# One decoder layer on one core: the last scores of the fourth attention group later, block two's probability transposes in two bursts, block two's MLP norm statistics ahead of the low parts

## The chip, the cores and the metric

The kernel runs on one core of a Trainium2 chip. The metric is the device time of one execution in microseconds (us), median over the runs. Three runs of the kernel before gave 1505.65, 1504.33 and 1505.69 us. The profiled execution took 1504.41 us, and its records span 1502.6 us from the first instruction to the last, so 1.8 us lie around the span.

Five engines work side by side, each through its own queue in order: PE multiplies matrices (its weight loads stand apart as PEld), DVE and ACT work on vectors, POOL is almost unused here, and SP starts transfers. What one needs from another it waits for at a semaphore.

## What is computed

One decoder layer in float32 on 256 tokens of width 2048. Around the change:

```python
h = rmsnorm(x, norm_mix_pre)
xr, yr, q, k, v, g_rnn, g_attn = split(h @ w_in)
y_att = sliding_window_sink_attention(rope(q), rope(k), v, sinks)   # 32 heads of 64, 4 key groups, window 128
mix = sigmoid(g_rnn) * (y_rnn @ w_rnn_proj) + sigmoid(g_attn) * (y_att @ w_attn_proj)
x = x + rmsnorm(mix @ w_out, norm_mix_post)
h = rmsnorm(x, norm_mlp_pre)
x = x + rmsnorm(square(relu(h @ w_mlp_up)) @ w_mlp_down, norm_mlp_post)
```

## The kernel before

**Tiling.** The 256 tokens are two blocks of 128 (`tb` 0 and 1). Float32 products are made of three products in a rounded format: each operand is split into a high part and a low part, and high by high, high by low and low by high are added. Weights stream in halves of 128x1024: SP loads `wraw` (4 buffers), ACT casts the high part `whi` (line 107, or 116 where it is issued by hand), DVE subtracts to get the low part `wlo` (line 108 or 124); `whi` and `wlo` have 6 buffers each. PE multiplies them with the activations: lines 307, 309 and 311 in the passes that keep tokens on the output's partitions, lines 267 and 269 in those that keep channels there (`a_pair`), line 952 for the last steps of `w_out`, line 1024 for the first steps of `w_mlp_up`.

**Attention between the projections.** For each of the four key groups `attention(g, banks)` is a generator. While PE runs the projections that follow, `pump()` is called after each half of weights (in `a_pair` four times a pair) and advances the oldest generator to its next `yield`. So each group's small steps lie between the large matmuls: `scores` (PE, line 579) into PSUM banks, `masked` (DVE, lines 591 and 593) which scales and masks them into SBUF and takes maxima, `exponents` (ACT, line 610), `shares` (DVE, lines 617 to 620) which divides by the sums, `turn_probs` (PE transposes, line 637, into banks `pt`, then ACT copies, line 639), and the product with the values (line 677, into `po`). Groups one to three run under the next group's passes; the fourth runs under `recur(0)`, the first channel passes of the recurrent branch (`conv` from line 738 and `gelu` from line 755, whose PSUM results are read by ACT at line 296 and DVE at line 297).

**Banks.** `pt` has the pool `psm` with two banks. `turn_probs(1)` fills four (two parities by two key blocks, four transposes each), so its third and fourth must wait for the ACT copies of the first two. In the first three groups the second block's scores have four banks; in the fourth, two of those are in use by the channel passes, and the second half of the scores must wait for `masked` to empty the pool `psb`.

**Before the MLP.** `w_out`'s result passes a norm, and `h2` must be transposed for `w_mlp_up`. For block one, then block two: `square` (ACT, line 920) sums squares, `gained` (DVE, line 923) applies gains, `norm` (lines 957 to 962: a reduce on DVE, a root on ACT, a reciprocal and four `h2` quarters on DVE), `turned` (PE transposes, line 968), `high` (ACT, line 973) and `low` (DVE, line 978). Block two's four transposed quarters share two banks, so the third waits until `high` and `low` of the first have read theirs. Meanwhile PE does block one's share of `w_mlp_up` (line 1024) with `whi` halves cast by hand (line 116).

**What sets the order.** A scheduler orders each engine's instructions at build time and the engines then run that fixed order. What is wrapped in `pin` keeps the order in which it was written.

Of the kernel before, what the change touches and what calls it, by code (L numbers as in the profile page):

```python
# [18 lines left out]
F32 = mybir.dt.float32  # L19
# [160 lines left out]
def layer(tc, x, x_t, few, pos_row, gains, w_kv, w_q, w_xy, w_rg, w_g, w_rp, w_ap, w_out,  # L180
# [43 lines left out]
    def unit(name, dt=F32R):  # L224
        return big.tile([P, 4, 2, S], dt, tag="U8", name=name)

    def flat(t):
        return t.rearrange("p a b c -> p (a b c)")

    ws = Stream(nc, wpool, chunks, lambda name: flat(unit(name, F32)), sums)  # L230
# [4 lines left out]
    def bank(pool, name):  # L235
        return pool.tile([P, 512], F32, tag=pool.name, name=name)
# [13 lines left out]
    def pair(name):  # L250

        pool = pairs[0]
        pairs.append(pairs.pop(0))
        return pool.tile([P, 2, 2, S], F32, tag="pair" + pool.name, name=name)
# [69 lines left out]
    def two_banks(name):  # L324
        room = pair(name)
        return [room[:, tb].rearrange("p a b -> p (a b)") for tb in range(TB)]
# [19 lines left out]
    def quarter(q):  # L346
        return slice(q * 512, q * 512 + 512)
# [203 lines left out]
    def attention(g, banks):  # L551
# [13 lines left out]
        rooms, stats, tiles = {}, {}, {}  # L565

        def scores(tb, j, both):

            w = P * (1 + tb)
            per = 512 // w  # L570
            if j == 0:
                rooms[tb] = flat(unit("s", F32)).rearrange("p (n c) -> p n c", c=512)
                stats[tb] = pa.tile([P, 4, 8], F32, tag="stat", bufs=3, name="stat")
                tiles[tb] = []
            for i in range(per):
                h = j * per + i
                for par in range(2):
                    r0 = par * HD
                    pin(mm(both[par][:, i * w : i * w + w], qT[r0 : r0 + HD, h, tb * P : tb * P + P],
                           kT[r0 : r0 + HD, g, 0:w], start=True, stop=True))  # L580
            return tb, j, both
# [40 lines left out]

        pT = {}

        def turn_probs(tb):
            nk = 1 + tb
            per = 4 // nk
            if tb:
                room_p = flat(unit("pT", F32)).rearrange("p (n c) -> p n c", c=512)
            else:  # L630
                room_p = rooms[tb][:, 2:4, :]
            for par in range(2):
                for kb in range(nk):
                    ps = bank(psm, "pt")
                    for h in range(4):
                        s3, at = tiles[tb][h // per * 2 + par]
                        nc.tensor.transpose(ps[:, h * P : h * P + P], s3[:, h % per, kb * P : kb * P + P], ident)
                    t = room_p[:, par * nk + kb, :]
                    nc.scalar.copy(t, ps)
                    pT[tb, par, kb] = t  # L640
# [11 lines left out]
        masked(*two)  # L652
        yield
        if last_group:
            three = scores(1, 1, [bank(psb, "sc") for par in range(2)])
            yield
        masked(*three)
# [6 lines left out]
        exponents(1, (2, 3))  # L664
        yield
        turn_probs(0)
        shares(1)
        yield
        yield
        turn_probs(1)  # L670
        yield
        yield
        for tb in range(TB):
            po = bank(psm, "po")
# [16 lines left out]
    for g in range(NKV):  # L691
        m1.append(pa.tile([P, TB, 512], F32, tag="m1", bufs=4, name=f"m1{g}"))
        for tb, b in enumerate(b_pass512(hT, two_banks("g"), 1)):
            nc.scalar.activation(m1[g][:, tb], b, AF.Tanh, scale=r0h[tb])
        waiting.append(attention(g, b_pass512(hT, [bank(psb, f"q{tb}") for tb in range(TB)], 1)))
# [220 lines left out]
    late = []  # L916
    h2T = units("h2T")

    def square(tb, q, b):
        pin(nc.scalar.activation(u2("j"), b, AF.Square, accum_out=sq[:, 1, tb, q : q + 1]))  # L920

    def gained(tb, q, b):
        pin(nc.vector.tensor_tensor(h2[tb][:, quarter(q)], b, gpg2[:, quarter(q)], ALU.mult))


    banks = [two_banks(f"o0{tb}") for tb in range(TB)]
# [17 lines left out]
    banks = [[bank(psb, f"o1{tb}{i}") for i in range(2)] for tb in range(TB)]  # L944
# [4 lines left out]
    def last_step(tb, i, kt, hi, lo):  # L949
        a, c = mixT[kt // 4][:, kt % 4], quarter(i)  # L950
        for x, w in ((0, hi), (0, lo), (1, hi)):
            pin(mm(banks[tb][i], a[:, x, tb * P : tb * P + P], w[:, c], start=False, stop=kt == KT - 1 and x == 1))

    def norm(tb):

        a, b = [st[:, 4 + 2 * tb + i : 5 + 2 * tb + i] for i in range(2)]
        pin(nc.vector.tensor_reduce(a, sq[:, 1, tb, :], AX.X, ALU.add))
        pin(nc.scalar.activation(b, a, AF.Sqrt, bias=eps, scale=1.0 / D))
        pin(nc.vector.reciprocal(a, b))
        for q in range(4):  # L960
            c = quarter(q)
            pin(nc.vector.scalar_tensor_tensor(h2[tb][:, c], h2[tb][:, c], a, xg[tb][:, c], ALU.mult, ALU.add))
        r1.append(a)

    def turned(tb, q):
        for i in range(4):
            k = 4 * q + i
            pin(nc.tensor.transpose(rooms[tb][q][:, i * P : i * P + P], h2[tb][:, k * P : k * P + P], ident))

    def high(tb, q):  # L970
        t = slice(tb * P, tb * P + P)
        p3 = rooms[tb][q].rearrange("p (a b) -> p a b", a=4)
        order["high"] = pin(nc.scalar.copy(h2T[q][:, :, 0, t], p3)).ins

    def low(tb, q):
        t = slice(tb * P, tb * P + P)
        p3 = rooms[tb][q].rearrange("p (a b) -> p a b", a=4)
        order["low"] = pin(nc.vector.tensor_tensor(h2T[q][:, :, 1, t], p3, h2T[q][:, :, 0, t].bitcast(F32),
                                                   ALU.subtract)).ins

    for i in range(2):
        for h in held:
            last_step(0, i, *h)
        square(0, 2 + i, banks[0][i])
        gained(0, 2 + i, banks[0][i])
    norm(0)
    for i in range(2):

        pin(nc.scalar.copy(og[:, 0, quarter(2 + i)], banks[0][i]))
    rooms = [[r[:, i].rearrange("p a b -> p (a b)") for r in (pair("ptr"), pair("ptr")) for i in range(2)],  # L990
             2 * [bank(psb, f"ptr{i}") for i in range(2)]]
# [5 lines left out]
    begun = [h[0] for h in halves]  # L997
    for h in range(2):
        last_step(1, 1, *held[2 * h])
        for q in (2 * h, 2 * h + 1):  # L1000
            turned(0, q)
        for q in (2 * h, 2 * h + 1):
            high(0, q)
        if h == 0:
            begun.append(ws.split_high())
        last_step(1, 1, *held[2 * h + 1])
        for q in (2 * h, 2 * h + 1):
            low(0, q)
        if h == 0:
            ws.split_low()  # L1010
    square(1, 3, banks[1][1])
    gained(1, 3, banks[1][1])
    begun.append(ws.split_high())
    norm(1)
    for j in range(2):
        begun.append(ws.split_high())


# [29 lines left out]
    for tb in range(TB):  # L1048
        for i in range(2):
            q = 2 + i  # L1050
# [146 lines left out]
    for f in range(2):  # L1197
        uT = {}
        rooms = [unit(f"uT{f}{i}") for i in range((PAIRS - len(SEVEN) + 1) // 2)]
# [48 lines left out]
        def between(p):  # L1248
            if p < 4:
                c = quarter(p)  # L1250
                nc.sync.dma_start(g3[:, c], gains[3][c].partition_broadcast(P))
            if p in (3, 5, 7, 9):
                tb, q = divmod((p - 3) // 2, 2)
                c = quarter(q)
                nc.vector.tensor_tensor(acc[tb][:, c], acc[tb][:, c], g3[:, c], ALU.mult)
# [27 lines left out]
        n = 0  # L1283
        down(f, n, uT, 2, order, finish, early)
        n = 1
# [82 lines left out]
```

## Time and profile before

| what | value |
|---|---|
| runs | 1505.65, 1504.33, 1505.69 us |
| profiled execution | 1504.41 us |
| its span | 1502.6 us |
| granted TensorE clock, mean | 0.997 |
| DVE busy | 1096.6 us (73%) |
| ACT busy | 829.9 us (55%) |
| PE's waits for other engines, summed by the view of waits | 4.9 us in 4 places |

The profile lists, for each instruction, its start from the span's beginning and its busy time. On PE the end of a matmul is modelled and runs into the next one, so the cost of a matmul is the distance from its start to the next start. "x8" merges eight instructions in a row. "Idle before" and an arrow name the engine, tile and line whose work ended the idle time.

### The profile page before, as it was taken

Reading aid. Unit: us, or ns where it says so; the run is one execution under the profiler, and the core shown is the slowest. Engines: PE = TensorE matmul, PEld = TensorE weight load, DVE = VectorE, ACT = ScalarE, POOL = GpSimd, SP = SyncE. Lnnn points to the kernel's source line nnn. Section 1 sums busy time; section 2 is a strip of 40 time slices with the busy share of each in tenths; the row PEclk is TensorE's granted clock in tenths of the full one; section 3 lists DMA queues with packets and bytes.
Section 4 is the critical chain, followed back from the end, with each engine's and each line's share of the span. In section 5 each row is a group of like instructions: output and inputs, shape, how many; then the busy total and the mean of one; then the engine's idle time right before and its main releaser. Section 6 shows DMA issues by size and latency. Waiting matters only on the chain.

```text
span 1502.6 us, 19925 instructions
## 1 busy us (share of the span) xinstructions
PE 1487.6 (99%) x7568; PEld 1259.3 (84%) x7568; DVE 1096.6 (73%) x1356; ACT 829.9 (55%) x1137; POOL 1.7 (0%) x9
## 2 busy tenths in 40 slices
PE   9999999999999999999999999999999999999997
PEld 7887787889889888888888888888888888888886
DVE  6576667858669966555758766798886666789897
ACT  8564664637566666443345654555454555455553
POOL 0000000000000000000000000000000000000000
PEclk9999999999999999999999999999999999999999
DMA  8644554565646566555764755566666565566665
GB/s 339 217 156 159 161 165 131 168 195 176 204 160 215 169 207 203 191 184 194 274 216 144 263 185 194 185 203 211 212 203 242 190 194 185 193 238 207 209 221 176
DMA packets 83471, 298.28 MB, mean 199 GB/s; under 512 B 9264, under 2 KB 9520, under 8 KB 82352
## 3 DMA queue, kind: packets, MB, share of 16 engines
q1 hardware_dynamic: 80064, 289.57, 58.3%
q10 hardware_dynamic: 3312, 7.45, 1.4%
q8 instruction: 59, 0.97, 0.2%
q14 instruction: 36, 0.29, 0.1%
HBM read 290.69 MB, written 6.29 MB: 198 GB/s over the span
## 4 chain that ended last, share of the span: by engine, by line
PE 97%; DVE 2%; ACT 1%; DMA 0%; issue 0%; DVEq 0%; SPq 0%; ACTq 0%
PE ps L269 22%; PE ps L267 12%; PE dQ L1131 9%; PE s L1131 5%; PE dP L1131 4%; PE g L307 4%; PE g L309 4%; PE g L311 4%; PE pp L309 4%; PE pp L307 4%; PE pp L311 4%; PE dCs L1131 3%; PE q L307 2%; PE q L311 2%; PE q L309 2%; PE o L311 2%
## 5 line engine op out<-in xcount | busy, mean ns | idle before, releaser
L108 DVE TENSOR_TENSOR wlo<-wraw,whi 128x1024 fp32r<-128x1024 f32 x516 | 624.2, 1220 | 312.1 <-ACT whi L107 309.5
L107 ACT CAST whi<-wraw 128x1024 fp32r<-128x1024 f32 x516 | 537.9, 1051 | 546.6 <-PE ps L269 132.1
L269 PE MATMUL ps<-h2T,whi 128*128 128x512 f32 x960 | 223.9, 390 | 0.0
L269 PEld LDWEIGHTS ps<-h2T,whi 128*128 128x128 f32 x960 | 178.2, 188 | 35.6
L267 PEld LDWEIGHTS ps<-h2T,wlo 128*128 128x128 f32 x960 | 119.1, 192 | 2.3
L269 PE MATMUL ps<-hT,whi 128*128 128x512 f32 x512 | 120.7, 391 | 0.0
L267 PE MATMUL ps<-h2T,wlo 128*128 128x256 f32 x960 | 119.9, 283 | 0.0
L269 PEld LDWEIGHTS ps<-hT,whi 128*128 128x128 f32 x512 | 94.7, 188 | 19.1 <-issue 0.3
L1131 PE MATMUL dQ<-whi,uT 128*128 128x512 f32 x288 | 106.8, 389 | 0.0
L307 PE MATMUL g<-whi,hT 128*128 128x512 f32 x256 | 101.1, 395 | 0.0
L311 PE MATMUL g<-whi,hT 128*128 128x512 f32 x256 | 99.8, 390 | 0.0
L309 PE MATMUL g<-wlo,hT 128*128 128x512 f32 x256 | 99.7, 390 | 0.0
L267 PEld LDWEIGHTS ps<-hT,wlo 128*128 128x128 f32 x512 | 63.8, 191 | 2.7 <-issue 1.5
L267 PE MATMUL ps<-hT,wlo 128*128 128x256 f32 x512 | 65.2, 284 | 0.0
L1131 PEld LDWEIGHTS dQ<-whi,uT 128*128 128x128 f32 x288 | 54.1, 188 | 11.2
L307 PEld LDWEIGHTS g<-whi,hT 128*128 128x128 f32 x256 | 48.1, 188 | 10.6 <-issue 1.0
L311 PEld LDWEIGHTS g<-whi,hT 128*128 128x128 f32 x256 | 48.1, 188 | 10.2
L309 PEld LDWEIGHTS g<-wlo,hT 128*128 128x128 f32 x256 | 48.1, 188 | 9.6
L1131 PE MATMUL dQ<-wlo,uT 128*128 128x512 f32 x144 | 56.0, 389 | 0.0
L1131 PE MATMUL dP<-whi,uT 128*128 128x512 f32 x144 | 54.1, 389 | 0.0
L1131 PE MATMUL dCs<-whi,uT 128*128 128x512 f32 x144 | 54.1, 389 | 0.0
L143 DVE TENSOR_TENSOR tlo<-t,thi 128x1536 fp32r<-128x1536 f32 x28 | 49.2, 1756 | 5.7 <-ACT thi L142 5.7
(284 smaller groups left out, 2466.5 us busy)
## 6 DMA issues: line engine op xcount, KB each, us to landing
wraw<-in_w_up SPq DMA_DIRECT2D x128, 512.0 KB, 4.1
wraw<-in_w_dn SPq DMA_DIRECT2D x128, 512.0 KB, 4.7
wraw<-in_w_g SPq DMA_DIRECT2D x64, 512.0 KB, 4.7
wraw<-in_w_xy SPq DMA_DIRECT2D x64, 512.0 KB, 3.9
wraw<-in_w_q SPq DMA_DIRECT2D x32, 512.0 KB, 4.1
wraw<-in_w_ap SPq DMA_DIRECT2D x32, 512.0 KB, 4.6
wraw<-in_w_rp SPq DMA_DIRECT2D x32, 512.0 KB, 4.0
wraw<-in_w_out SPq DMA_DIRECT2D x32, 512.0 KB, 4.8
```

Source lines behind the costliest of these rows:

```text
L107: self.pin(self.nc.scalar.copy(hi, src))
L108: self.pin(self.nc.vector.tensor_tensor(lo, src, hi.bitcast(F32), ALU.subtract))
L143: v.tensor_tensor(lo, t, hi.bitcast(F32), ALU.subtract)
L267: mm(ps[:, f, 1, :], w, a[:, 0, :], start=False, stop=j == 1 and k == 7)
L269: mm(ps[:, f].rearrange("p a b -> p (a b)"), w, a.rearrange("p a b -> p (a b)"), start=kt == 0, stop=j == 3 and k == 7)
L307: mm(banks[tb][n], a[:, 0, t], hi[:, n * 512 : n * 512 + 512], start=first, stop=False)
L309: mm(banks[tb][n], a[:, 0, t], lo[:, n * 512 : n * 512 + 512], start=False, stop=False)
L311: mm(banks[tb][n], a[:, 1, t], hi[:, n * 512 : n * 512 + 512], start=False, stop=last)
L1131: mm(b, a[x], w[y], start=not begun and i == 0, stop=tail and i == 2)
```

## The change

Three edits. In the fourth group one more `yield` stands ahead of the last scores. `turn_probs(1)` becomes two calls, one for each parity, with a `yield` between; this holds in all four groups, and the number of yields after it falls by one. Before the MLP, `norm(1)` is given two callbacks: the reduce and the root come ahead of the last `low` of block one, and the last `gained` of block two comes ahead of the last quarter of `h2` alone; the cast that stood ahead of `norm(1)` follows it.

```diff
-        def turn_probs(tb):
+        def turn_probs(tb, pars=(0, 1)):
             nk = 1 + tb
             per = 4 // nk
-            if tb:
-                room_p = flat(unit("pT", F32)).rearrange("p (n c) -> p n c", c=512)
-            else:
-                room_p = rooms[tb][:, 2:4, :]
-            for par in range(2):
+            if tb and 0 in pars:
+                rooms["pT"] = flat(unit("pT", F32)).rearrange("p (n c) -> p n c", c=512)
+            room_p = rooms["pT"] if tb else rooms[tb][:, 2:4, :]
+            for par in pars:
...
         if last_group:
+            yield
             three = scores(1, 1, [bank(psb, "sc") for par in range(2)])
             yield
         masked(*three)
...
-        turn_probs(1)
-        yield
+        turn_probs(1, (0,))
+        yield
+        turn_probs(1, (1,))
         yield
...
-    def norm(tb):
+    def norm(tb, between=None, late=None):
         a, b = [st[:, 4 + 2 * tb + i : 5 + 2 * tb + i] for i in range(2)]
         pin(nc.vector.tensor_reduce(a, sq[:, 1, tb, :], AX.X, ALU.add))
         pin(nc.scalar.activation(b, a, AF.Sqrt, bias=eps, scale=1.0 / D))
+        if between:
+            between()
         pin(nc.vector.reciprocal(a, b))
         for q in range(4):
             c = quarter(q)
+            if q == 3 and late:
+                late()
             pin(nc.vector.scalar_tensor_tensor(h2[tb][:, c], h2[tb][:, c], a, xg[tb][:, c], ALU.mult, ALU.add))
...
-        for q in (2 * h, 2 * h + 1):
-            low(0, q)
+        low(0, 2 * h)
         if h == 0:
+            low(0, 1)
             ws.split_low()
     square(1, 3, banks[1][1])
-    gained(1, 3, banks[1][1])
-    begun.append(ws.split_high())
-    norm(1)
-    for j in range(2):
+    norm(1, lambda: low(0, 3), lambda: gained(1, 3, banks[1][1]))
+    for j in range(3):
         begun.append(ws.split_high())
```

In the first three groups the second burst of eight transposes (line 636 in the new numbering) now stands twelve projection matmuls behind the first, where before two pieces of four stood three and four matmuls behind it.

**The fourth group's last scores on PE** (`sc`, between channel matmuls with low weights at line 267 and high weights at line 269). Before:

```order
L267 MATMUL ps<-hT_150,wlo_2094 128x256 x2
L579 MATMUL sc<-kT,qT_2115 128x256
L267 MATMUL ps<-hT_150,wlo_2094 128x256
L579 MATMUL sc<-kT,qT_2115 128x256 x3
L267 MATMUL ps<-hT_150,wlo_2094 128x256
L267 MATMUL ps<-hT_147,wlo_2133 128x256 x4
L267 MATMUL ps<-hT_148,wlo_2133 128x256 x4
```

Now:

```order
L267 MATMUL ps<-hT_150,wlo_2094 128x256 x4
L267 MATMUL ps<-hT_147,wlo_2133 128x256 x4
L267 MATMUL ps<-hT_148,wlo_2133 128x256 x4
L267 MATMUL ps<-hT_149,wlo_2160 128x256 x4
L267 MATMUL ps<-hT_150,wlo_2160 128x256 x4
L579 MATMUL sc<-kT,qT_2115 128x256 x4
L269 MATMUL ps<-hT_147,whi_2132 128x512 x3
```

The four scores stand together, eighteen line-267 matmuls later than the first stood.

**The fourth group's transposes for block two**, on PE (`pt`) and on ACT (the copies `pT`, lines 639 before and 638 now; `u` and `xct` are the activation of `gelu`, lines 757 and 759 before, 758 and 760 now). PE now; before, the two bursts of eight had a single line-269 matmul between them:

```order
L269 MATMUL ps<-hT_150,whi_2385 128x512 x4
L636 MATMUL pt<-ident,s 128x128 x8
L269 MATMUL ps<-hT_147,whi_2422 128x512
L267 MATMUL ps<-hT_147,wlo_2346 128x256 x4
L267 MATMUL ps<-hT_148,wlo_2346 128x256 x4
L267 MATMUL ps<-hT_149,wlo_2386 128x256
L636 MATMUL pt<-ident,s 128x128 x8
```

ACT before:

```order
L296 COPY py<-ps 128x512
L639 COPY pT<-pt 128x512 x2
L107 CAST whi_2536<-wraw_2395 128x1024
L639 COPY pT<-pt 128x512 x2
L107 CAST whi_2567<-wraw_2430 128x1024
L757 ACTIVATE u<-py 128x512
```

ACT now:

```order
L296 COPY py<-ps 128x512
L107 CAST whi_2511<-wraw_2389 128x1024
L107 CAST whi_2555<-wraw_2426 128x1024
L107 CAST whi_2581<-wraw_2444 128x1024
L758 ACTIVATE u<-py 128x512
L638 COPY pT<-pt 128x512 x2
L760 ACTIVATE xct<-u 128x512
L638 COPY pT<-pt 128x512 x2
```

Both pairs of copies have moved behind the activation of `gelu` and the three casts ahead of it.

**Block two's norm on DVE** (`st` the sum of squares, `h_6168` block two's `h2`, `h2T` the low parts). Before:

```order
L978 TENSOR_TENSOR h2T_6179<-ptr,h2T_6179 128x4x128
L978 TENSOR_TENSOR h2T_6180<-ptr,h2T_6180 128x4x128
L923 TENSOR_TENSOR h_6168<-o_6491,gpg_6160 128x512
L957 TENSOR_REDUCE st<-sqs 128x1
L959 RECIPROCAL st<-st 128x1
L962 SCALAR_TENSOR_TENSOR h_6168<-h_6168,st,xg_6166 128x512 x4
L978 TENSOR_TENSOR h2T_6177<-ptr_6753,h2T_6177 128x4x128
```

Now:

```order
L983 TENSOR_TENSOR h2T_6179<-ptr,h2T_6179 128x4x128
L958 TENSOR_REDUCE st<-sqs 128x1
L983 TENSOR_TENSOR h2T_6180<-ptr,h2T_6180 128x4x128
L962 RECIPROCAL st<-st 128x1
L967 SCALAR_TENSOR_TENSOR h_6168<-h_6168,st,xg_6166 128x512 x3
L924 TENSOR_TENSOR h_6168<-o_6491,gpg_6160 128x512
L967 SCALAR_TENSOR_TENSOR h_6168<-h_6168,st,xg_6166 128x512
L983 TENSOR_TENSOR h2T_6177<-ptr_6753,h2T_6177 128x4x128
```

The reduce has moved ahead of one low part and of line 923's gain, and that gain now stands among the four quarters, still ahead of block two's first low part.

## The prediction

> **What bounds the kernel.** I read the page's busy times first, then the totals of the view of waits.
>
> ```profile
> PE 1487.6 (99%) x7568; PEld 1259.3 (84%) x7568; DVE 1096.6 (73%) x1356; ACT 829.9 (55%) x1137; POOL 1.7 (0%) x9
> ```
>
> PE is busy for 1487.6 of 1502.6 us; all other engines follow it. The change removes no matmul. What it can win is time in which PE stands, or turns between kinds of matmul. PE's view of waits names the places:
>
> ```profile
> PE sc L579 <- DVE s L591: 1.1, 1, 1.1
> PE ptr L968 <- DVE h L962: 0.7, 1, 0.7
> ...
> PEld pt L637 <- ACT pT L639: 2.0, 4, 0.5
> ...
> DVE wlo L108 <- ACT whi L107: 309.5, 200, 3.6
> ```
>
> Each edit aims at one of the first three rows (the fourth is used below): the fourth group's scores, the norm's transposes, and the bursts of probability transposes, once in each group. A busy share hides part of the loss, so I measure each place from start to start. For that I need the plain matmuls' pace, from the chain in order of time:
>
> ```profile
> 261.91 7.28 PE ps L269 x32
> ...
> 357.69 3.83 PE ps L267 x32
> ```
>
> So a 512-column matmul takes 0.227 us and a 256-column one 0.12 us.
>
> **Part one: bursts.** PE's timeline in group one:
>
> ```profile
> 110.82 1.03 PE L637 MATMUL pt<-ident,s 128*128 128x128 f32 x8
> 111.61 0.48 PE L307 MATMUL q<-whi,hT 128*128 128x512 f32 x1
> 111.92 0.40 PE L309 MATMUL q<-wlo,hT 128*128 128x512 f32 x1
> 112.16 0.40 PE L311 MATMUL q<-whi,hT 128*128 128x512 f32 x1
> 112.65 0.66 PE L637 MATMUL pt<-ident,s 128*128 128x128 f32 x4
> 113.06 0.48 PE L307 MATMUL q<-whi,hT 128*128 128x512 f32 x1
> 113.37 0.60 PE L637 MATMUL pt<-ident,s 128*128 128x128 f32 x4
> 113.73 0.48 PE L309 MATMUL q<-wlo,hT 128*128 128x512 f32 x1
> 114.04 0.39 PE L311 MATMUL q<-whi,hT 128*128 128x512 f32 x1
> ```
>
> The first, clean burst costs 110.82 to 111.92 less one matmul: 1.10 - 0.23 = 0.88 us, of which 0.09 is the slower first matmul behind it (0.31 instead of 0.23). All sixteen transposes cost 3.22 less five matmuls (1.14), or 2.08 us. Two clean bursts cost 1.76, so 0.33 us are saved. The new second burst comes twelve matmuls (2.7 us) after the first; two copies at 0.5 to 0.6 us each end well before, and the cast now between the copies is hidden too, so no bank is missed in groups one to three. Group four's two bursts:
>
> ```profile
> 277.16 1.03 PE L637 MATMUL pt<-ident,s 128*128 128x128 f32 x8
> ...
> 279.38 0.70 PE L269 MATMUL ps<-hT,whi 128*128 128x512 f32 x2
> ```
>
> 2.22, plus 0.09 for the slower matmul behind, less one matmul: 2.08 again. Sum over four groups: **1.32 us**, if no new wait arises.
>
> **Part two: scores.**
>
> ```profile
> 255.74 0.76 PE L267 MATMUL ps<-hT,wlo 128*128 128x256 f32 x5
> 257.63 0.70 PE L579 MATMUL sc<-kT,qT 64*128 64x256 f32 x2 [1.13 <-DVE s L591]
> 258.25 0.38 PE L267 MATMUL ps<-hT,wlo 128*128 128x256 f32 x1
> 258.57 1.13 PE L579 MATMUL sc<-kT,qT 64*128 64x256 f32 x6
> 259.62 2.29 PE L267 MATMUL ps<-hT,wlo 128*128 128x256 f32 x17
> ```
>
> Four scores are eight records, which can run in pairs, one on each half of the array's rows. The fifth line-267 matmul starts at 255.74 + 4 x 0.12 = 256.22. From there to 259.62 are 3.40 us, with two such matmuls (0.24) in it; with the slower return (0.1) the four scores and their wait cost 3.26. The second visit does six records, some of them singly, in 1.05; eight in pairs need the same four slots, and with entry and return (0.1 each) one visit costs 1.27 by my estimate. PE now asks at 256.22 + 19 x 0.12 = 258.50, and 0.09 later, after the turn, the second bank has been free, since PE wrote it at 258.57. So **1.98 us** are saved; were the records not paired, two slots of 0.21 more would be needed and 1.56 saved. The later scores delay nobody: DVE reduced them at 263.35, over 3 us after they were done.
>
> **Part three: what the copies' new place costs.** This is the step against the change. PE's second burst in group four needs the two `pt` banks that the first burst filled, and the copies that free them now stand on ACT behind `u<-py`. That waits for DVE's `py` times `rT` (line 755), the last in a long queue:
>
> ```profile
> 263.35 1.26 DVE L593 TENSOR_REDUCE stat<-s 128x2 f32<-128x512 f32 x2
> ...
> 267.49 1.29 DVE L620 TENSOR_TENSOR s<-s,stat 128x512 f32<-128x512 f32 x2
> 268.69 1.22 DVE L108 TENSOR_TENSOR wlo<-wraw,whi 128x1024 fp32r<-128x1024 f32 x1
> 269.83 2.44 DVE L745 SCALAR_TENSOR_TENSOR xct<-px,tiny,xct 128x255 f32<-128x255 f32 x6
> 272.19 0.16 DVE L617 TENSOR_TENSOR stat<-stat 128x8 f32<-128x8 f32 x1
> ...
> 272.62 0.69 DVE L620 TENSOR_TENSOR s<-s,stat 128x512 f32<-128x512 f32 x1
> ```
>
> Slots from start to start: a 512-column operation 0.60 (two from 267.49 to 268.69), a low part 1.14, the six of line 745 2.36, lines 617 and 618 0.43. The queue starts at 263.35 + 1.2 = 264.55 (the first cast it needs waits for PE, which comes 2 us earlier). From there to line 755 the new order has six low parts (6.84), ten 512-column operations (6.0), line 745 (2.36), twice 617 and 618 (0.86) and three small ones (0.2): 16.3 us. Line 755 starts at 280.8 and, at 0.69 each, ends at 281.5. ACT then:
>
> ```profile
> 277.84 1.08 ACT L639 COPY pT<-pt 128x512 f32<-128x512 f32 x2
> ...
> 282.23 0.63 ACT L757 ACTIVATE u<-py 128x512 f32<-128x512 f32 x1
> ```
>
> The activation takes 281.5 to 282.1, the first copy ends about 282.65, PE starts at 282.7. PE itself arrives earlier: its line-269 matmuls, which began at 259.62 + 17 x 0.12 + 0.1 = 261.75, begin at 259.77, then 7.28 + 3.83 + 0.88 (block one's burst) + 31 x 0.227 + 0.88 + (0.23 + 9 x 0.12) = 280.98. It stands for 1.7 us, and 0.06 more at the restart (112.65: 0.66 for four against 0.60 at 113.37): **-1.76 us**. (The first three groups move both queues alike, by 1.0.) Bounds: nothing, if DVE's queue is 1.7 us quicker than its slots; 3.3, if one of its low parts waits for a cast as long as the mean of the 200 waits, 309.5/200 = 1.5. I take the sum of the slots, since none of the quoted rows carries an idle note. Behind the waiting transposes stand 23 line-267 matmuls and `po`; nobody else is short, since `po` is read by the attention projection only after 72 matmuls (16 us). The second copies and `po`, now 24 matmuls later, lie beside PE.
>
> **Part four: norm.**
>
> ```profile
> 803.79 3.28 PE L1024 MATMUL ps<-h2T,whi 128*128 128x256 f32 x26
> 804.50 1.28 DVE L978 TENSOR_TENSOR h2T<-ptr,h2T 128x512 fp32r<-128x512 f32 x2
> 807.00 2.74 DVE L962 SCALAR_TENSOR_TENSOR h<-h,st,xg 128x512 f32<-128x512 f32 x4
> 807.80 0.66 PE L968 MATMUL ptr<-ident,h 128*128 128x128 f32 x4 [0.73 <-DVE h L962]
> 809.65 1.30 DVE L978 TENSOR_TENSOR h2T<-ptr,h2T 128x512 fp32r<-128x512 f32 x2
> 810.39 0.66 PE L968 MATMUL ptr<-ident,h 128*128 128x128 f32 x4
> ```
>
> PE asks for the first quarter at 803.79 + 26 x 0.12 = 806.91 and gets it at 807.80. Now the reduce follows one low part, at 805.1; the root, on ACT, runs under the second, whose slot ends at 805.76; the quarters start at 805.96, the first ends at 806.7, and that wait is gone (0.89). But the third burst of transposes needs the bank that block two's first low part reads, and ahead of that still stand three quarters (to 807.95), the gain (0.61) and the fourth quarter (0.66): it starts at 809.22 and ends at 809.9. PE asks at 806.91 + 2 x 1.15 = 809.2 and starts at 809.95 instead of 810.39. The stall has moved from the first burst to the third: **0.44 us** won. Bounds: 0 and 1.12, if that stall too is hidden. The weight cast that now follows the root (ready at about 806.55) is needed at the 24th of the 26 matmuls, 806.67; a late one would cost tenths.
>
> **Sum:** 1.32 + 1.98 - 1.76 + 0.44 = 1.98 us. Against the profiled 1504.41 that is 1502.4; the runs' median lies 1.24 higher, and from it I get 1503.7.
>
> **Rivals.** *No new stall* (DVE or ACT gets there in time): 1505.65 - 3.74 = 1501.9. For it: ACT is busy 55%. Against: the queue's order is fixed, and DVE's sum leaves 1.7 us missing.
>
> *The clock drops.* Two stretches at the start, with PE's busy time and its granted clock:
>
> ```profile
> 4.90:8.30 3.40, 1.38 (x8) 1.00 1.01 393
> 8.30:11.70 3.40, 3.40 (x10) 0.50 1.03 400
> ```
>
> After a stretch in which PE was busy for 1.38 of 3.40 us, the next ran at half clock. The new stall leaves about 1.7 of 3.4, with eight transposes in it. If 3.4 us run at half clock, 1.7 us are lost: 1505.4. Against: the scores' wait of 1.13 us was no such case. The Trainium skill (TensorE: Matmul & The Clock Gate, Part 4: PE-mode transpose) says that transposes do not count as busy; by that the stall and its burst are 2.5 us without activity. The same page (Why this matters for your kernels) warns only of idle gaps over about 3 us, and by that the clock stays.
>
> *Slower: the last cast ahead of `u<-py` waits for its load.*
>
> ```profile
> wraw<-in_w_ap SPq DMA_DIRECT2D x32, 512.0 KB, 4.6
> ```
>
> It is issued when the fourth low part of the new queue frees a buffer, about 275.5; landed 4.6 us later and cast in 1.05 it is done at 281.2, 0.3 before the activation is due. From a landing time of 6.9 us on, the stall outweighs all gains; at 9 us the kernel takes 1507.8. Against: that is double the median.
>
> **How the numbers follow.** Forecast 0.58 (1503.7, own range 1502.7 to 1504.7); no new stall 0.24; clock 0.10; load 0.08. About 0.2% (3.0 us) is what a measurement can tell from no change. Faster by more, below 1502.64: most of the second case and a tenth of the first, 0.28. Slower, above 1508.66: half of the last, 0.05. Within: 0.67. The range of 1501.2 to 1505.5 holds the first two cases with part four's better bound, and the clock's; it leaves out the load's and the outer ends.
>
> **What would show it.** The changed profile should have no wait of `sc`, three unbroken bursts of eight transposes in each group, a wait of PE for ACT at line 638 of about 1.7 us near 281, and at the norm a wait for line 983 in place of line 967's. If the first is absent the time is near 1502; if the granted clock shows a half-speed stretch behind it, near 1505.

## The result, and the profile after

The changed kernel took 1502.40 us (median of 15 runs, 1500.83 to 1503.73), the kernel before 1504.72 us (15 runs, 1502.84 to 1506.03). The ratio is 0.9982 with a 95% interval of 0.9976 to 0.9989: a gain of 0.18%. The interval leaves out 1, so the gain is real, but it lies inside the 0.2% that was called no change. The forecast was 1503.7 us with a range of 1501.2 to 1505.5. The profiled execution took 1502.42 us, with a span of 1500.6 us.

The page's busy times after:

```profile
PE 1485.3 (99%) x7568; PEld 1259.0 (84%) x7568; DVE 1097.8 (73%) x1356; ACT 829.6 (55%) x1137; POOL 1.7 (0%) x9
```

PE's view of waits after (waited for, total us, times, longest):

```profile
PE kv L415 <- ACT hT L402: 2.5, 1, 2.5
PE pt L636 <- ACT pT L638: 1.4, 1, 1.4
PE warm L396 <- DVE ones L380: 1.1, 1, 1.1
PE ptr L973 <- DVE h2T L983: 0.7, 1, 0.7
```

Against before, `sc` is gone, the transposes at line 636 now wait for ACT's copies, and the norm's wait is for line 983's low part, no longer for line 967's (before 962's) quarter. Neither total says what each place is worth; for that the starts of the same matmuls are laid side by side, place by place.

**The places on PE.** Each column is a stretch between two matmuls that both kernels have, and says by how many us it is shorter than in the profile of before. The first row is the forecast, the second the change; the others are the experiments below.

| | start, to 14 us | bursts, groups one to three | scores of group four | its bursts and stall | norm | behind it | PE in all |
|---|---|---|---|---|---|---|---|
| forecast | – | 0.99 | 1.98 | 0.33 - 1.76 = -1.43 | 0.44 | – | 1.98 |
| the change | 0.12 | 0.97 | 1.97 | -1.34 | 0.31 | 0.00 | 2.02 |
| scores_only | 0.13 | -0.04 | 1.99 | -1.34 | 0.02 | 0.00 | 0.78 |
| bursts_only | 1.58 | 0.99 | -0.04 | 0.15 | 0.04 | -0.03 | 2.69 |
| norm_only | 0.30 | -0.02 | 0.00 | -0.02 | 0.35 | 0.01 | 0.62 |
| copies_first | 0.32 | 0.99 | 1.97 | -0.75 | 0.36 | 0.01 | 2.89 |
| copies_ahead | 0.18 | 0.97 | 1.97 | 0.32 | 0.32 | -0.23 | 3.51 |
| longer_stall | 1.43 | 0.96 | 1.97 | -1.41 | 0.32 | 0.01 | 3.28 |
| low_first | 0.06 | 0.99 | 1.97 | -1.35 | 1.12 | -0.43 | 2.35 |
| both_ahead | 0.36 | 0.99 | 1.97 | 0.32 | 1.12 | -0.13 | 4.62 |
| norm_stall | -0.08 | 0.96 | 1.97 | -1.34 | -5.30 | -0.01 | -3.79 |
| both_warm | 1.71 | 0.96 | 1.97 | 0.32 | 1.12 | -0.11 | 5.97 |

A burst, score or norm place that a kernel doesn't touch repeats to within 0.04 us. The stretch behind the norm does so in seven kernels of eleven; in the other four PE lost 0.11 to 0.43 there. The start varies by 1.7 us between profiles of the same ten warm-ups, and the stretch behind PE's last matmul varies by 1.5 (both in the last section). The experiments are therefore read by place, and a single time of theirs is not.

**Bursts.** PE's timeline in group one after (start, duration, engine, line, operation, count):

```profile
110.72 1.03 PE L636 MATMUL pt<-ident,s 128*128 128x128 f32 x8
111.51 0.48 PE L307 MATMUL q<-whi,hT 128*128 128x512 f32 x1
...
114.33 1.04 PE L636 MATMUL pt<-ident,s 128*128 128x128 f32 x8
115.12 0.47 PE L307 MATMUL q<-whi,hT 128*128 128x512 f32 x1
```

Two unbroken bursts of block two, 0.79 us each until the next matmul, twelve matmuls between them, and no wait.

**Scores and the new stall.** PE's timeline in group four after:

```profile
257.53 1.14 PE L579 MATMUL sc<-kT,qT 64*128 64x256 f32 x8
258.59 3.74 PE L269 MATMUL ps<-hT,whi 128*128 128x512 f32 x15
...
278.89 1.23 PE L267 MATMUL ps<-hT,wlo 128*128 128x256 f32 x9
281.51 1.14 PE L636 MATMUL pt<-ident,s 128*128 128x128 f32 x8 [1.39 <-ACT pT L638]
282.40 2.99 PE L267 MATMUL ps<-hT,wlo 128*128 128x256 f32 x23
```

All eight records stand in one visit of 1.06 us, in pairs, with no wait. The second burst is asked for at 278.89 + 9 x 0.12 = 279.97 and starts at 281.51. What it waits for stands in ACT's timeline, and what ACT waits for in DVE's:

```profile
278.52 1.06 ACT L107 CAST whi<-wraw 128x1024 fp32r<-128x1024 f32 x1 [1.21 <-DMA wraw<-in_w_ap]
280.35 0.63 ACT L758 ACTIVATE u<-py 128x512 f32<-128x512 f32 x1 [0.77 <-DVE py L756]
280.88 1.05 ACT L638 COPY pT<-pt 128x512 f32<-128x512 f32 x2
```

```profile
278.50 1.22 DVE L108 TENSOR_TENSOR wlo<-wraw,whi 128x1024 fp32r<-128x1024 f32 x1
279.63 0.69 DVE L756 TENSOR_TENSOR py<-py,rT 128x512 f32<-128x512 f32 x1
```

DVE has no idle note on any row from 263.47 to the end of line 756 at 280.32; then the activation, then the copies, then PE. The last cast had ended at 279.58, 0.77 us before the activation could start: its load was not what decided. And the clock (stretches of 3.4 us around the stall; PE busy, then further engines, then granted clock, DMA share, GB/s):

```profile
278.50:281.90 3.40, 2.01 (x17) 1.77 (x15) 2.71 (x5) 2.61 (x5) 0.00 (x0) 1.00 0.68 201
281.90:285.30 3.40, 3.40 (x30) 3.23 (x28) 2.76 (x3) 1.53 (x4) 0.00 (x0) 1.00 0.62 218
```

It stayed at 1.00, and the matmuls of line 267 behind the burst start 0.12 us apart, the pace of before.

**Norm.** DVE's timeline after, then PE's:

```profile
804.25 2.08 DVE L967 SCALAR_TENSOR_TENSOR h<-h,st,xg 128x512 f32<-128x512 f32 x3
806.25 0.68 DVE L924 TENSOR_TENSOR h<-o,gpg 128x512 f32<-128x512 f32 x1
806.97 0.75 DVE L967 SCALAR_TENSOR_TENSOR h<-h,st,xg 128x512 f32<-128x512 f32 x1
807.63 1.28 DVE L983 TENSOR_TENSOR h2T<-ptr,h2T 128x512 fp32r<-128x512 f32 x2
```

```profile
805.22 0.60 PE L973 MATMUL ptr<-ident,h 128*128 128x128 f32 x4
...
808.37 0.66 PE L973 MATMUL ptr<-ident,h 128*128 128x128 f32 x4 [0.70 <-DVE h2T L983]
```

The first burst starts without a wait, the third waits for the low part that starts at 807.63.

### The profile page after: what moved, and what is told of

It reads as the page before. It is cut to its first block, busy times and chain, and to the rows that moved or that the text cites. A ratio compares the mean times of both kernels' runs of the same rounds, so it can differ in the third digit from the quotient of the medians.

```text
span 1500.6 us, 19926 instructions
## 1 busy us (share of the span) xinstructions
PE 1485.3 (99%) x7568; PEld 1259.0 (84%) x7568; DVE 1097.8 (73%) x1356; ACT 829.6 (55%) x1137; POOL 1.7 (0%) x9
## 4 chain that ended last, share of the span: by engine, by line
PE 97%; DVE 2%; DMA 0%; ACT 0%; issue 0%; DVEq 0%; SPq 0%; ACTq 0%
PE ps L269 22%; PE ps L267 12%; PE dQ L1134 9%; PE s L1134 5%; PE dP L1134 4%; PE g L307 4%; PE g L311 4%; PE g L309 4%; PE pp L309 4%; PE pp L307 4%; PE pp L311 4%; PE dCs L1134 3%; PE q L307 2%; PE q L311 2%; PE q L309 2%; PE o L307 2%
```

## The experiments

**One part at a time.** scores_only is the kernel before with this alone:

```diff
         if last_group:
+            yield
             three = scores(1, 1, [bank(psb, "sc") for par in range(2)])
```

> Only the scores of group four are moved; bursts and norm as before. Mine (the later scores alone put the probability copies behind `u<-py`): no wait for `sc`, the scores' place 1.97 us shorter, and in group four PE stands 1.4 to 1.7 us for ACT at the probability transposes near 282; with the 0.33 of a second burst that now comes ten matmuls after the first, the place around it loses 1.3. Nothing in groups one to three, the norm's wait of 0.7 stays. Net 0.5 to 0.7 us below before. Rival (the split of the bursts is what delays the copies): no such wait of PE, net 2.0 to 2.3.

Measured: 1.99 at the scores and -1.34 at the stall, as in the whole change, though the transposes are not split in its code. PE's timeline there:

```profile
282.47 1.14 PE L637 MATMUL pt<-ident,s 128*128 128x128 f32 x8 [1.39 <-ACT pT L639]
```

The stall comes with the later scores. Two thirds of what they win is lost 24 us later, and what remains is 0.65.

bursts_only is the kernel before with the two hunks of `turn_probs` and its calls:

```diff
-        turn_probs(1)
-        yield
+        turn_probs(1, (0,))
+        yield
+        turn_probs(1, (1,))
         yield
```

> Only the bursts are split. Mine: 0.33 us in each of groups one to three and again in group four, no wait of the transposes of group four (the first copies stand ahead of `u<-py` there), the wait for `sc` of 1.1 and the norm's 0.7 stay. The second pair of copies stands behind `u<-py`, so `po` may wait for up to 0.45. Net 0.9 to 1.3. Rival (the split delays the copies): PE waits about 1.5 us at the second burst of group four, net about -0.2.

Measured: 0.99 in the first three groups and 0.15 in group four, with no wait of PE at its transposes. Its two bursts on PE, and on ACT the first copies ahead of the activation:

```profile
274.63 1.03 PE L636 MATMUL pt<-ident,s 128*128 128x128 f32 x8
...
279.15 1.03 PE L636 MATMUL pt<-ident,s 128*128 128x128 f32 x8
```

```profile
275.31 1.08 ACT L638 COPY pT<-pt 128x512 f32<-128x512 f32 x2
...
279.23 0.63 ACT L757 ACTIVATE u<-py 128x512 f32<-128x512 f32 x1 [0.64 <-DVE py L755]
...
281.23 1.05 ACT L638 COPY pT<-pt 128x512 f32<-128x512 f32 x2
```

So the split does not delay the first copies, and both bursts are clean. Group four gains 0.18 us less than the others because the second pair of copies does stand behind the activation: the product with the values (`po`, line 677) takes the banks that these copies free. The first of the two ends at 281.80, and PE's weight load for the product starts right behind it:

```profile
281.85 0.20 PEld L677 LDWEIGHTS po<-s,v_sb 128*64 128x64 f32 x4 [0.34 <-ACT pT L638]
```

Eleven matmuls of line 267 stand ahead of it from 280.26 on; at 0.12 us each, and with 0.08 for the turn as in the kernel before, the product could have started at 281.66, 0.19 us earlier. The view of waits does not list it for PE, whose own idle time there is only 0.13 us.

norm_only is the kernel before with the change's hunks behind line 950, of which this is the end:

```diff
...
-    gained(1, 3, banks[1][1])
-    begun.append(ws.split_high())
-    norm(1)
-    for j in range(2):
+    norm(1, lambda: low(0, 3), lambda: gained(1, 3, banks[1][1]))
+    for j in range(3):
```

> Only the norm is changed. Its part does not touch the others: the waits for `sc` (1.1) and none at the transposes of group four as before, the first burst of the norm without a wait, the third with 0.7 for the add that frees its bank; net 0.31 us, as in the whole change (0.44 was forecast). Rival (what is ahead of it shifts the norm's wait): another size than 0.31 by over 0.1.

Measured: 0.35 at the norm, nothing elsewhere. The three parts alone add up to 0.65 + 1.14 + 0.35 = 2.14 us, the change's own four places to 1.91: they are independent but for group four's bursts, which lose 0.18 to the second copies when they are split alone; in the change these copies are done 1.9 us before the product.

**The copies' place on ACT.** copies_first is the change with

```diff
-                    nc.scalar.copy(t, ps)
+                    with tc.high_priority(PRIO) if tb and last_group else ExitStack():
+                        nc.scalar.copy(t, ps)
```

which puts group four's first two copies ahead of `u<-py` and behind the last cast.

> The whole change, and in group four the first two copies of block two's probabilities stand ahead of `u<-py` on ACT, behind the last weight cast. Mine (the copies wait behind `u<-py` for the end of DVE's queue): the wait of 1.4 at the transposes falls to 0.2, and the kernel gains 1.3 us on the change, to a span near 1499.3. Rival (the load of that last cast sets the stall): the copies still stand behind that cast, so the wait stays near 1.4 and the time at the change's. Rival (the clock): nothing shown at full granted clock before or after, no loss beyond the stall.

Measured: the place improved by 0.59 us only, from -1.34 to -0.75, where 1.3 had been expected. ACT's timeline, and PE's burst:

```profile
278.99 1.05 ACT L107 CAST whi<-wraw 128x1024 fp32r<-128x1024 f32 x1 [1.91 <-DMA wraw<-in_w_ap]
279.94 1.06 ACT L639 COPY pT<-pt 128x512 f32<-128x512 f32 x2
280.89 0.64 ACT L759 ACTIVATE u<-py 128x512 f32<-128x512 f32 x1
```

```profile
280.57 1.14 PE L636 MATMUL pt<-ident,s 128*128 128x128 f32 x8 [0.80 <-ACT pT L639]
```

The copies no longer wait for DVE, and then the load shows: the cast ahead of them waited 1.91 us for it. The expectation was wrong in taking the cast's end from the change's profile, where the load came 0.7 us sooner against PE's own place. Two things hold the copies, one behind the other, DVE's queue and the load.

copies_ahead therefore puts them ahead of the cast too: the first two copies are also pinned, and

```diff
         turn_probs(1, (1,))
+        if last_group:
+            ws.pin = pin
         yield
+        ws.pin = lambda i: i
```

pins the cast, which is written later, so that it stands behind them (it lands behind the tanh).

> The whole change, and in group four the first two probability copies stand ahead of the last weight cast too, not of `u<-py` alone. Mine (two things behind each other hold the copies: first DVE's queue, and 0.6 to 0.8 us before it the load of that cast): no wait of PE for the copies at all, the place 1.4 to 1.5 us shorter than in the change; the cast, now behind the tanh, has over 60 matmuls until it is used and makes no new wait. Rival (PE is held there by something else, its own turn or the product's bank): the wait stays above 0.5. Rival (the later cast delays loads): a new wait at the attention projection.

Measured: no wait of PE for the copies. PE's timeline:

```profile
278.83 1.11 PE L267 MATMUL ps<-hT,wlo 128*128 128x256 f32 x8
279.78 1.03 PE L636 MATMUL pt<-ident,s 128*128 128x128 f32 x8
280.57 3.11 PE L267 MATMUL ps<-hT,wlo 128*128 128x256 f32 x24
```

The place goes from -1.34 to +0.32, by 1.66 us: that is the whole price of the stall, which the forecast had put at 1.76, and what is left is its 0.33 for clean bursts. The idle note of 1.39 falls 0.27 short of that price, since the modelled end of the matmul ahead covers part of the wait and the restart is slower. The later cast made no wait of PE in the view; the 0.23 us that PE lost near 1440 us in this profile were not followed up.

longer_stall was meant to try the clock: one of those first two copies five times over.

```diff
-                    nc.scalar.copy(t, ps)
+                    for again in range(5 if tb and last_group and not par and not kb else 1):
+                        nc.scalar.copy(t, ps)
```

> The whole change, with one of the first two copies done five times over in group four, so that PE stands longer. Mine (the stall costs its own length as long as PE keeps the full clock): PE stands 2.4 to 3.0 us in place of 1.4, the place is longer by about that difference, the granted clock stays 1.00. Rival (idle time of this size drops the clock): a stretch of about 3.4 us at half clock behind the stall, 1 to 1.7 us more than the stall's own growth.

It missed. The scheduler moved PE's transposes apart and most of the repeated copies behind the next activation, PE still stood for 1.4 us (-1.41 at the place), and nothing follows for the clock.

**The norm's third burst.** low_first is the change with the fourth quarter handed back by `norm` and run behind block two's first low part, and with the third weight cast behind it:

```diff
-    norm(1, lambda: low(0, 3), lambda: gained(1, 3, banks[1][1]))
-    for j in range(3):
+    last_quarter = norm(1, lambda: low(0, 3), lambda: gained(1, 3, banks[1][1]))
+    for j in range(2):
...
+        if q == 0:
+            last_quarter()
+            begun.append(ws.split_high())
```

> The whole change, but at the norm block two's first low part stands ahead of the norm's fourth quarter on DVE, and the third of the weight casts behind it on ACT. Mine (the third burst of transposes waits only for the bank that this low part frees): the wait of 0.7 there nearly goes, the place is 0.6 to 0.75 us shorter than in the change, and the fourth quarter is in time for the fourth burst. Rival (the fourth quarter or the cast is what the bursts wait for): the wait moves to the fourth burst or to the cast's first matmul, gain under 0.2.

Measured: the place gains 1.12 us on before, 0.81 more than the change, somewhat above what was expected. 1.12 is also the upper bound that the prediction gave this part, though the rows that it quotes (810.39 less 809.2) make that bound 1.19. At 1329 us PE lost 0.43 to a wait for DVE's `u` that the change doesn't have; both_ahead, with the same edit, doesn't have it either.

**All of it.** both_ahead is copies_ahead and low_first, with both edits as shown above.

> copies_ahead and low_first together. Mine: their gains add, 2.0 to 2.2 us below the change and 4.0 to 4.3 below before from the first group on (a ratio of 0.997); of PE's waits only the two at the start are left. Rival (waits taken away here come back later): less than 1 us below the change.

Measured: 4.62 us on PE against before and 2.60 against the change, of which 0.24 is the start; the other 2.36 are a little more than was expected. Its view of waits for PE has only the two at the start:

```profile
PE kv L415 <- ACT hT L402: 2.0, 1, 2.0
PE warm L396 <- DVE ones L380: 1.1, 1, 1.1
```

In time: 1500.86 us (11 runs, 1498.58 to 1502.61) against 1504.70 for before (15 runs), a ratio of 0.9973, with an interval of 0.9964 to 0.9982. This beats before; that it beats the change is shown on PE's places, while the two ratios' intervals just overlap.

**The clock.** norm_stall lengthens the wait at the norm, where the order is pinned. The gain is done five times over, with the same values:

```diff
             if q == 3 and late:
-                late()
+                for again in range(5):
+                    late()
```

> The whole change, with the gain of block two's last quarter done five times over, each time with the same values, ahead of the norm's fourth quarter: PE's wait at the third burst grows from 0.7 by four operations of 0.6 each to 3.1 us. Mine (a stall in mid-kernel costs its own length): the place is 2.4 us longer than in the change, the granted clock stays 1.00 behind it. Rival (idle time of this size drops the clock, as after 1.8 to 2.5 us at the start): a stretch of about 3.4 us at half clock behind it, up to 1.7 us more, 4.1 in all.

Measured: the place is 5.61 us longer than in the change. DVE's timeline, PE's row, and stretches of 3.4 us with PE's busy time first and the granted clock third from the end:

```profile
806.43 3.58 DVE L924 TENSOR_TENSOR h<-o,gpg 128x512 f32<-128x512 f32 x5
810.05 0.75 DVE L968 SCALAR_TENSOR_TENSOR h<-h,st,xg 128x512 f32<-128x512 f32 x1
```

```profile
811.46 1.11 PE L974 MATMUL ptr<-ident,h 128*128 128x128 f32 x4 [3.59 <-DVE h2T L984]
```

```profile
808.80:812.20 3.40, 0.74 (x4) 0.74 (x5) 3.33 (x6) 0.00 (x0) 0.00 (x0) 0.78 0.00 0
812.20:815.60 3.40, 3.40 (x18) 3.40 (x17) 1.86 (x3) 1.17 (x2) 0.00 (x0) 0.50 0.31 107
815.60:819.00 3.40, 3.40 (x23) 3.40 (x23) 3.40 (x5) 0.53 (x1) 0.00 (x0) 0.72 0.36 86
```

Four more operations took (810.05 - 806.43) / 5 x 4 = 2.90 us, not 2.4. The other 2.7 is the clock: the shares of half speed in the three rows (0.22, 0.50 and 0.28 below full, doubled, times 3.4) come to 1.5 + 3.4 + 1.9 = 6.8 us. The rival holds, and at 2.7 us in place of the 1.7 at most that it had named: two stretches of 3.4 us at half clock, not one. It is one profile of one such stall.

The Trainium skill (TensorE: Matmul & The Clock Gate, Why this matters for your kernels) warns of gaps over some 3 us. The 3.59 us here agree, and so do the 1.39 us of the change, which cost no clock; the 1.9 to 2.5 us at the start (last section) do not.

both_warm is both_ahead with more warm-ups:

```diff
-WARM = 10
+WARM = 16
```

> both_ahead, with 16 in place of 10 warm-up matmuls at the start, so that PE is idle there for 0.5 to 1.2 us instead of 1.6 to 2.5. Mine (idle time of that size at the start is what drops the clock in most runs, and that is most of the spread between runs): no half-clock stretch behind it, 1.0 to 1.4 us below both_ahead, and a narrower spread. Rival (the clock's drop at the start comes from something else, such as a clock that was not yet full): the half-clock stretch stays, no gain; or the last warm-ups themselves delay the first real matmul by some tenths.

Measured: PE was not idle at all ahead of line 415, where 0.5 to 1.2 us had been expected, the first real matmuls ran at full pace, and the start is 1.35 us shorter than in both_ahead. Two of the eleven profiles with ten warm-ups start as fast (last section), so this one profile does not show that the six warm-ups did it. PE's timeline:

```profile
1.08 6.20 PE L396 MATMUL warm<-ones 128*128 128x128 f32 x32 [1.08 <-DVE ones L380]
7.19 1.25 PE L415 MATMUL kv<-whi,hT 128*128 128x512 f32 x4
```

The kernel took 1499.94 us (5 runs, 1498.74 to 1501.04) against 1505.41 for before (9 runs): 0.9963, with an interval of 0.9950 to 0.9977. It is the lowest median that was measured, but this interval and both_ahead's overlap for most of their length, and its profile gives the gain back at the end (below). The runs spread over 2.3 us in five, against 4.0 in both_ahead's eleven, too few to call the spread narrower.

## Why the prediction was right, point by point

- **Bursts:** 0.33 us a group were forecast, 0.97 were measured for three, and 0.32 for the fourth once the stall was out of the way. Reading the price from one clean burst held.
- **Scores:** 1.98 forecast, 1.97 measured. The records do run in pairs, and the bank was free when PE asked.
- **The stall:** 1.76 forecast, 1.66 measured. Summing DVE's slots gave the place: line 756 was to end 281.5 - 1.0 (the first three groups' gain) = 280.5, and ended at 280.32. What the prediction did not say is which edit puts the copies there. It is the scores' move alone; the order of ACT is not tied to the split of the bursts.
- **Norm:** 0.44 forecast, 0.31 measured. The mechanism was right, a size was off: the gain of line 924 took a slot of 0.72 us, not 0.61, since the quarter behind it reads what it has just written.
- **The total:** the sum, 1.98 us, gives 1502.4 from the profiled 1504.41, and the profiled execution after took 1502.42. That it meets so closely is luck: the four places make 1.91 us, 0.12 come from the start, which no edit touches, and the runs of one kernel spread over 3 us. From the medians the gain is 2.32. The forecast of 1503.7 started from a median of three runs, 1505.65, that was 0.93 above the median of fifteen; the result lies 0.3 below the likeliest case's own range for that reason, inside the wide one.
- **The rivals:** "no new stall" falls by the wait of 1.4 alone: its time of 1501.9 lies nearer to the measured 1502.40 than the forecast's 1503.7, so without the profile the time would have spoken for the wrong mechanism. "The clock" fell in this kernel (1.00 around the stall) and was seen as a mechanism, at a longer stall, in norm_stall. "The load" did not decide here, by 0.77 us; copies_first shows it deciding as soon as DVE's queue no longer does.

## What to carry to other kernels

Price a moved step by the queue that it lands behind, on the engine where its consumers' buffers are freed: here a wait of 1.1 us was removed and one of 1.4 appeared 24 us later, on another engine's account, because a scheduler put two copies behind an activation. Here the sum of the slots of a queue that has no idle notes foretold such a wait to 0.1 us. When the first holder is taken away, look for the second one right behind it before counting the whole wait as won.

## What the runs showed of the hardware

**A half-clock start, by chance.** In eleven profiles with ten warm-ups PE is idle for 1.6 to 2.5 us ahead of line 415, and three things happen.

- In seven (idle for 1.9 to 2.5 us) the steps between the warm-ups had begun to shorten from 0.21 towards 0.11 us before the idle time: the clock had risen (in the prediction's rows for the kernel before it is granted 1.00 in the stretch from 4.90 us, and 0.50 in the next). Behind it seven or eight of the next dozen 512-column matmuls start 0.41 to 0.59 us apart, most of them 0.43, in place of 0.23.
- In scores_only and copies_ahead (1.8) the warm-ups kept their 0.21 us to the end, and seven of the next matmuls are as slow: the full clock had not yet come. The view of stretches reads 1.00 even there, so at the start the pace is the surer sign.
- In bursts_only (1.6) and longer_stall (1.8) the warm-ups kept their 0.21 us too, and yet the real matmuls run at full pace at once. That is the 1.4 us or so by which these two stand out in the table's column for the start.

So 1.8 us of idle time stand ahead of a slow start and of a fast one, and its length alone does not decide. The Trainium skill (TensorE: Matmul & The Clock Gate, What's actually happening) has a free-running window of about 3.4 us behind this, and an idle window that brings the half clock back. The chance agrees with it; that the idle time has to fill such a window does not, since gaps of 1.9 to 2.5 us were enough in the seven.

**A dependence costs 0.12 us on DVE.** The 128x512 operation of line 924 takes a slot of 0.72 us where the next operation reads or rewrites its result (the change, norm_stall), and 0.60 where it doesn't, in both_ahead's timeline of DVE:

```profile
804.32 0.69 DVE L930 TENSOR_TENSOR h<-o,gpg 128x512 f32<-128x512 f32 x1
804.92 0.68 DVE L992 TENSOR_TENSOR h2T<-ptr,h2T 128x512 fp32r<-128x512 f32 x1
```

**The end is not always PE's.** From PE's last start to the end of the span are 10.0 us in the change, 10.1 in both_ahead, 11.7 in both_warm and 11.5 in scores_only. The page's chain that ended last is 97% PE in the change and 99% in both_ahead. In both_warm:

```profile
PE 91%; DVE 4%; DMA 3%; ACT 1%; issue 1%; DVEq 0%; ACTq 0%
```

This chain runs through loads of `in_w_dn`, the last of them 7.09 us long, behind whose cast DVE's last sums stand. PE's gain is not what decides it: scores_only and norm_stall have such a chain too (PE 85% and 91%), with a PE that ends later than both_ahead's, and norm_stall's end, 11.3 us behind PE's last start, is among the longest. Why these loads come late in some profiles and not in others was not found. A gain on PE is therefore not yet a gain in the time of one run: both_warm is 1.35 us ahead of both_ahead on PE's last start and 0.4 behind in the span.
